# Feed-forward: the up projection as seven half-size products, and the down projection as a stage of its own

## The chip, the cores and the metric

One Trainium2 chip, one core. The metric is the device time of one execution in microseconds (us). TensorE is called PE in the profile, VectorE DVE, ScalarE ACT, GpSimd POOL; SP only starts DMAs. Every engine runs its own queue of instructions in order and waits on semaphores.

## The reference

One layer of a streaming encoder: attention with a compressed key/value cache, retention, and a feed-forward part. Only the last is touched. On 1152 tokens (1024 of one prompt, 8 x 16 of samples) of 1024 features, with 2816 hidden features:

```python
h = rms_norm(x, w['g_norm_ffn'])
u = h @ w['w_ffn_up']                       # 1024 -> 2 * 2816
# causal depthwise convolution over time, width 3, with bias, on all 5632 columns
gate, value = halves of the convolved u
x = x + (silu(gate) * value) @ w['w_ffn_down']   # 2816 -> 1024
```

The state of the convolution (the last two rows of `u` of the prompt and of each sample) is read and returned.

## The kernel before

Features lie on the 128 partitions, tokens along the free axis. A product in full precision is made of three products of rounded halves (`mm3`: high x high, high x low, low x high), so each weight tile and each activation row is split once by `split`: ScalarE casts to the high half (L205), VectorE subtracts (L206).

Attention, retention and the input projections come first. Then three layers of 8 output tiles each, `w_or`, `w_oa` and `w_out`, give the residual `xf[0..7]` (`ret_out`, `att_out`, `res_out`). Then the feed-forward part, a loop over 22 pairs `j`: gate tile `j` and value tile `22 + j`. For each of the two tiles:

- `up_mm` makes 3 token chunks x 8 k tiles x 3 = 72 products of 384 columns into three PSUM banks;
- `up_in` multiplies the sums by the norm's reciprocal root (row `iv2b`) as VectorE reads them out of PSUM (L1228, L1229), while POOL copies the convolution state in and out (L1224, L1225, L1230, L1231);
- `conv` starts on ScalarE (L1235) and takes two multiply-adds on VectorE (L1236, L1238), silu for the gate on ScalarE (L1240).

VectorE multiplies gate and value (L1305), the result is split into `ah` and `al`, and stays in SBUF. When two pairs are there, `down` multiplies them with their rows of `w_dn`: 8 output tiles x 3 chunks x 2 pairs x 3 products of 384 columns, each sum added to `xf` by VectorE (L1254, 264 additions). `down` for earlier pairs stands between the gate and the value products of a later one.

The order on each engine is that of the code as a scheduler of the tile framework lays it out by the dependencies; pools with a number of buffers set how far loads run ahead. Weights are loaded on SP's queue into `wraw`.

Of the kernel before, what the change touches and what calls it, by code (L numbers as in the profile page):

```python
# [8 lines left out]
F32 = mybir.dt.float32  # L9
F32R = mybir.dt.float32r  # L10
# [66 lines left out]
def _lay_out(x):  # L77
# [53 lines left out]
    o["w_dn"] = asc(a["w_ffn_down"][0].reshape(NJ, P, D))  # L131
# [41 lines left out]
def _body(tc, d):  # L173
# [37 lines left out]
    with ExitStack() as top:  # L211
        const = top.enter_context(pool("const"))
        dram = top.enter_context(pool("dram", space=bass.MemoryType.DRAM))
        wp = top.enter_context(pool("wp", bufs=4))
# [18 lines left out]
        s_r8 = scratch("s_r8", RH, (P, 256 + 2 * RV))  # L233
        stream = _Stream()
# [895 lines left out]
        rp = top.enter_context(pool("rrows", side=right))  # L1130

        def new_rows(mm, w, f0, f1, fill):
            wts = [wslot(d[w][f], D) for f in (f0, f1)]
            rows = []

            def row(k):
                hi = rp.tile([P, T], F32R, name="rh", tag=f"rh{k}")
                lo = rp.tile([P, T], F32R, name="rl", tag=f"rl{k}")
                fill(k, hi, lo)
                rows.append((hi, lo))  # L1140
                return hi, lo

            return rows, fm_pair(mm, wts, row)

        def layer(mm, w, n, fill, out):
            rows, first = new_rows(mm, w, 0, 1, fill)
            for f in range(n):
                out(f, fm_tile(mm, wslot(d[w][f], D), rows) if f > 1 else first[f])

        NU = 2 + SEQ + NB * (NS + 2)  # L1150
        fs = top.enter_context(pool("frows"))
        fw = top.enter_context(pool("fconv"))
        with ExitStack() as ph:
            mm = top.enter_context(pool("mm_f", bufs=6, space=PSUM))
            sm = top.enter_context(pool("sm_f", bufs=2, space=PSUM))
            wk = ph.enter_context(pool("mwork", bufs=2, side=right))
            ivb = rp.tile([P, T], F32, name="iv2b")
            xf = []

            def ret_out(f, ps):  # L1160
                xf.append(fs.tile([P, T], F32, name=f"xf{f}"))
                g = wk.tile([P, T], F32, name="mg")
                G.dma_start(g, s_gate[8 + f])
                for c in range(NCH):
                    cs = slice(c * CH, (c + 1) * CH)
                    V.tensor_tensor(out=xf[f][:, cs], in0=ps[c], in1=g[:, cs], op=ALU.mult)

            def att_out(f, ps):
                g = wk.tile([P, T], F32, name="mg")
                G.dma_start(g, s_gate[f])  # L1170
                for c in range(NCH):
                    cs = slice(c * CH, (c + 1) * CH)
                    V.tensor_tensor(out=g[:, cs], in0=ps[c], in1=g[:, cs], op=ALU.mult)
                    V.tensor_tensor(out=xf[f][:, cs], in0=xf[f][:, cs], in1=g[:, cs], op=ALU.add)

            acc = fw.tile([P, NU - 2], F32, name="cv")[:, :T]

            def res_out(f, ps):
                g = wk.tile([P, T], F32, name="mg")
                G.dma_start(g, d["x_fm"][f])  # L1180
                for c in range(NCH):
                    cs = slice(c * CH, (c + 1) * CH)
                    V.tensor_tensor(out=xf[f][:, cs], in0=ps[c], in1=g[:, cs], op=ALU.add)
                if f:
                    A.activation(g, xf[f], AF.Square)
                    V.tensor_tensor(out=acc, in0=acc, in1=g, op=ALU.add)
                else:
                    A.activation(acc, xf[f], AF.Square)

            layer(mm, "w_or", 8, lambda k, hi, lo: split(hi, lo, raw(s_ret[k], T)), ret_out)  # L1190
            layer(mm, "w_oa", 8, lambda k, hi, lo: split(hi, lo, raw(s_att[k], T)), att_out)
            layer(mm, "w_out", 8, lambda k, hi, lo: split(hi, lo, xf[k]), res_out)


            hr, (pg, pv) = new_rows(mm, "w_up", 0, NJ, lambda k, hi, lo: split(hi, lo, xf[k], gc(C_FFN, k)))


        with ExitStack() as ph:
            wk = ph.enter_context(pool("fwork", bufs=1))
            cn = cst("s_conv", (P, NF, 18), wk)  # L1200

            def up_mm(f):
                return fm_tile(mm, wslot(d["w_up"][f], D), hr)

            def up_raw(ps):
                u = wk.tile([P, NU], F32, name="u", bufs=2)
                us = u[:, 2 + SEQ:].rearrange("p (b c) -> p b c", b=NB)
                A.copy(u[:, 2:2 + CH], ps[0])
                V.tensor_copy(u[:, 2 + CH:2 + 2 * CH], ps[1])
                n = SEQ - 2 * CH  # L1210
                A.copy(u[:, 2 + 2 * CH:2 + SEQ], ps[2][:, :n])
                V.tensor_copy(us[:, :, 2:], ps[2][:, n:].rearrange("p (b i) -> p b i", b=NB))
                return u

            def up_in(f, ps, u=None):
                if u is None:
                    u = wk.tile([P, NU], F32, name="u", bufs=2)
                    us = u[:, 2 + SEQ:].rearrange("p (b c) -> p b c", b=NB)
                    tail = ps[2][:, SEQ - 2 * CH:].rearrange("p (b i) -> p b i", b=NB)
                else:  # L1220
                    us = u[:, 2 + SEQ:].rearrange("p (b c) -> p b c", b=NB)
                    ps = [u[:, 2 + c * CH:2 + (c + 1) * CH] for c in range(3)]
                    tail = us[:, :, 2:]
                G.tensor_copy(u[:, 0:2], cn[:, f, 0:2])  # L1224
                G.tensor_copy(us[:, :, 0:2], cn[:, f, 2:].rearrange("p (b i) -> p b i", b=NB))  # L1225
                for c in range(3):
                    n = min(CH, SEQ - c * CH)
                    V.tensor_tensor(out=u[:, 2 + c * CH:2 + c * CH + n], in0=ps[c][:, :n], in1=ivb[:, c * CH:c * CH + n], op=ALU.mult)  # L1228
                V.tensor_tensor(out=us[:, :, 2:], in0=tail, in1=ivb[:, SEQ:].rearrange("p (b i) -> p b i", b=NB), op=ALU.mult)  # L1229
                G.tensor_copy(cn[:, f, 0:2], u[:, SEQ:SEQ + 2])  # L1230
                G.tensor_copy(cn[:, f, 2:].rearrange("p (b i) -> p b i", b=NB), us[:, :, NS:])  # L1231
                return u

            def conv(f, u, c):
                A.activation(c, u[:, 2:], AF.Identity, scale=gc(C_CW, 2 * NF + f), bias=gc(C_CB, f))  # L1235
                V.scalar_tensor_tensor(out=c, in0=u[:, 1:NU - 1], scalar=gc(C_CW, NF + f), in1=c, op0=ALU.mult, op1=ALU.add)  # L1236
                yield 1
                V.scalar_tensor_tensor(out=c, in0=u[:, 0:NU - 2], scalar=gc(C_CW, f), in1=c, op0=ALU.mult, op1=ALU.add)  # L1238
                if f < NJ:
                    A.activation(c, c, AF.Silu)  # L1240

            def down(acts, wd, last):
                for f in range(8):
                    wts = [tuple(w[:, f * P:(f + 1) * P] for w in ww) for ww in wd]
                    if last and f == 7:
                        ps = [mm.tile([P, 512], F32, name="mm")[:, :CH] for _ in range(NCH)]
                    else:
                        ps = fm_tile(mm, wts, acts)
                    for c in range(NCH):
                        cs = slice(c * CH, (c + 1) * CH)  # L1250
                        if last and f == 7:
                            for k in range(2):
                                mm3(ps[c], wts[k], tuple(a[:, cs] for a in acts[k]), k == 0, k == 1)
                        V.tensor_tensor(out=xf[f][:, cs], in0=ps[c], in1=xf[f][:, cs], op=ALU.add)  # L1254
                        if last:
                            S.dma_start(d["y_fm"][f][:, cs], xf[f][:, cs])

            acts, wd = [], []
            held = [up_raw(p) for p in (pg, pv)]
            i2 = const.tile([P, NT], F32, name="i2")  # L1260

            def norm():
                V.tensor_scalar(out=ss, in0=col_sums(sm, acc), scalar1=1.0 / D, scalar2=EPS, op0=ALU.mult, op1=ALU.add)
                rpow(i2, ss)
                yield from to_rows(sm, ivb, i2, fw.tile([P, NU - 2], F32, name="cg")[:, :CH])

            def act_rows(cv, ah, al):
                split(ah[:, :SEQ], al[:, :SEQ], cv[:, :SEQ])
                sv = lambda a: a[:, SEQ:].rearrange("p (b i) -> p b i", b=NB)
# [3 lines left out]
            def down_w(j):  # L1273
                return wslot(d["w_dn"][j], D)
# [95 lines left out]
```

## Time and profile before

| | |
|---|---|
| median of 3 runs | 2465.95 us (2463.95 to 2468.12) |
| profiled execution | 2464.82 us; span 2463.0 us; granted clock 0.992 |
| PE busy | 2435.9 us, 99% of the span |
| DVE, ACT, POOL busy | 1319.5, 835.8, 302.3 us |
| bytes moved by DMA | 238.52 MB, mean 97 GB/s |

A busy time is the sum of an engine's instructions, not the time it was needed for. A group row reads: line, engine, operation, output <- inputs, shape, number; then total busy us and mean ns of one; then idle time of that engine ahead of the group and who ended it. A row of the chain reads: start, length, what ran, number of instructions. A row of the timeline reads: start, length, engine, line, operation.

### The profile page before, as it was taken

Reading aid. Unit: us, or ns where it says so; the run is one execution under the profiler, and the core shown is the slowest. Engines: PE = TensorE matmul, PEld = TensorE weight load, DVE = VectorE, ACT = ScalarE, POOL = GpSimd, SP = SyncE. Lnnn points to the kernel's source line nnn. Section 1 sums busy time; section 2 is a strip of 40 time slices with the busy share of each in tenths; the row PEclk is TensorE's granted clock in tenths of the full one; section 3 lists DMA queues with packets and bytes.
Section 4 is the critical chain, followed back from the end, with each engine's and each line's share of the span. In section 5 each row is a group of like instructions: output and inputs, shape, how many; then the busy total and the mean of one; then the engine's idle time right before and its main releaser. Section 6 shows DMA issues by size and latency. Waiting matters only on the chain.

```text
span 2463.0 us, 36197 instructions
## 1 busy us (share of the span) xinstructions
PE 2435.9 (99%) x14360; PEld 2333.8 (95%) x14360; DVE 1319.5 (54%) x2779; ACT 835.8 (34%) x2050; POOL 302.3 (12%) x514
## 2 busy tenths in 40 slices
PE   9999999999999999999999999999999999999999
PEld 9999998998999978887999999999999999999999
DVE  5223456456249856444886244247555555555555
ACT  5121332333236645664665022133221222212120
POOL 0001000001013302332110000011110101110010
PEclk9999999999999999998999999999999999999999
DMA  5332210220126576427764352210111111111102
GB/s 200 103 110 102 95 60 27 69 65 29 69 77 181 171 250 204 146 101 204 195 187 128 113 165 90 93 60 30 48 44 43 44 43 35 52 44 43 43 26 84
DMA packets 125273, 238.52 MB, mean 97 GB/s; under 512 B 10000, under 2 KB 73872, under 8 KB 124848
## 3 DMA queue, kind: packets, MB, share of 16 engines
q1 hardware_dynamic: 40320, 125.95, 15.6%
q10 hardware_dynamic: 58256, 62.30, 7.5%
q0 software_dynamic: 26528, 47.95, 7.0%
q8 instruction: 113, 1.85, 0.3%
q14 instruction: 56, 0.46, 0.1%
HBM read 168.76 MB, written 67.42 MB: 96 GB/s over the span
## 4 chain that ended last, share of the span: by engine, by line
PE 94%; DVE 3%; ACT 1%; DMA 1%; issue 1%; POOL 0%; ACTq 0%; SPq 0%; DVEq 0%; POOLq 0%
PE mm L188 81%; PE sm L188 4%; PE sc L188 3%; PE apo L188 2%; PE apt L1081 1%; DVE wlo L206 0%; DMA s<-s_ret 0%; PE sm L554 0%; DVE uqT L697 0%; DMA wraw<-w_gate 0%; PE sm L311 0%; PE sm L691 0%; PE sm L859 0%; DVE uqT L209 0%; PE sm L987 0%
## 5 line engine op out<-in xcount | busy, mean ns | idle before, releaser
L205 ACT CAST whi<-wraw 128x1024 fp32r<-128x1024 f32 (+2 forms) x165 | 172.3, 1053 | 725.8 <-PE mm L188 629.6
L188 PE MATMUL mm<-rh,whi 128*128 128x384 f32 x1728 | 392.7, 336 | 1.5 <-ACT rh L205 1.5
L188 PE MATMUL mm<-rh,wlo 128*128 128x384 f32 x1680 | 384.1, 336 | 0.0
L188 PE MATMUL mm<-rl,whi 128*128 128x384 f32 x1632 | 372.5, 336 | 0.1
L188 PEld LDWEIGHTS mm<-rh,whi 128*128 128x128 f32 x1728 | 308.1, 188 | 3.2 <-ACT rh L205 1.7
L188 PEld LDWEIGHTS mm<-rh,wlo 128*128 128x128 f32 x1680 | 300.2, 188 | 0.0
L188 PEld LDWEIGHTS mm<-rl,whi 128*128 128x128 f32 x1632 | 291.0, 188 | 0.4 <-DVE rl L206 0.4
L206 DVE TENSOR_TENSOR wlo<-wraw,whi 128x1024 fp32r<-128x1024 f32 (+2 forms) x165 | 200.1, 1222 | 142.1 <-ACT whi L205 142.0
L188 PE MATMUL mm<-whi,xh 128*128 128x256 f32 (+2 forms) x720 | 228.2, 333 | 0.7 <-DVE gsig L361 0.7
L188 PE MATMUL mm<-whi,xl 128*128 128x256 f32 (+2 forms) x720 | 225.3, 329 | 0.0
L188 PE MATMUL mm<-wlo,xh 128*128 128x256 f32 (+2 forms) x720 | 224.8, 329 | 0.2 <-DVE wlo L206 0.2
L1254 DVE TENSOR_TENSOR xf<-mm,xf 128x384 f32<-128x384 f32 x264 | 131.5, 551 | 86.2 <-PE mm L188 86.2
L1228 DVE TENSOR_TENSOR u<-mm,iv2b 128x384 f32<-128x384 f32 (+1 forms) x126 | 57.1, 507 | 208.9 <-PE mm L188 208.9
L188 PEld LDWEIGHTS mm<-whi,xl 128*128 128x128 f32 x720 | 132.5, 190 | 12.1
L188 PEld LDWEIGHTS mm<-whi,xh 128*128 128x128 f32 x720 | 132.6, 190 | 10.6 <-issue 0.7
L188 PEld LDWEIGHTS mm<-wlo,xh 128*128 128x128 f32 x720 | 132.6, 190 | 9.8 <-DVE wlo L206 0.4
L188 PE MATMUL mm<-xh,whi 128*128 128x384 f32 x528 | 123.9, 340 | 2.8 <-ACT whi L205 2.1
L188 PE MATMUL mm<-xl,whi 128*128 128x384 f32 x528 | 122.1, 337 | 0.0
L188 PE MATMUL mm<-xh,wlo 128*128 128x384 f32 x528 | 121.5, 336 | 0.0
L188 PE MATMUL mm<-ah,whi 128*128 128x384 f32 x480 | 110.4, 336 | 0.0
L188 PE MATMUL mm<-al,whi 128*128 128x384 f32 x480 | 110.4, 336 | 0.0
L188 PE MATMUL mm<-ah,wlo 128*128 128x384 f32 x480 | 109.7, 336 | 0.0
(448 smaller groups left out, 4449.0 us busy)
## 6 DMA issues: line engine op xcount, KB each, us to landing
wraw<-w_up SPq DMA_DIRECT2D x44, 512.0 KB, 3.2
s_q<-uqT ACTq DMA_DIRECT2D x36, 384.0 KB, 3.1
aq<-s_q POOLq DMA_DIRECT2D x8, 1536.0 KB, 9.1
wraw<-w_dn SPq DMA_DIRECT2D x22, 512.0 KB, 3.3
s_gate<-gsig ACTq DMA_DIRECT2D x16, 576.0 KB, 4.9
mg<-s_gate POOLq DMA_DIRECT2D x16, 576.0 KB, 5.0
wraw<-w_rqkv SPq DMA_DIRECT2D x16, 512.0 KB, 3.6
s_v<-kvT ACTq DMA_DIRECT2D x16, 512.0 KB, 4.6
```

The lines of the kernel that those rows point to most:

```text
L188: E.matmul(out, l, r, start=start, stop=stop)
L205: A.copy(hi, src)
L206: return V.tensor_tensor(out=lo, in0=src, in1=hi.bitcast(F32), op=ALU.subtract)
L1081: E.transpose(pt[:, j * 256 + e * P:j * 256 + (e + 1) * P], pm[e][:, jj * P:(jj + 1) * P], ident)
L1228: V.tensor_tensor(out=u[:, 2 + c * CH:2 + c * CH + n], in0=ps[c][:, :n], in1=ivb[:, c * CH:c * CH + n], op=ALU.mult)
L1254: V.tensor_tensor(out=xf[f][:, cs], in0=ps[c], in1=xf[f][:, cs], op=ALU.add)
```

## The change

Only the part from `w_or` on is changed, and the layout of `w_dn`.

**Up projection.** For one pair, gate and value tile are the two row blocks of a 2 x 2 block product; the 8 k tiles are halved into the two inner blocks, the 1152 tokens into two halves of 576. The four blocks of the result then come from seven products of half size (the Winograd form of Strassen's scheme) instead of eight: 7 products x 2 chunks of 288 columns x 4 k tiles x 3 = 168 products per pair (before: 144 of 384 columns). Three pairs of PSUM banks `p`, `q`, `r` hold the sums. A bank that has been read goes on summing the next product, and the reads in between give the four blocks (`read`). Four sums of weight blocks per pair are made by POOL (`up_w`); the sums of token blocks are made once, behind `w_out` (`res_out`, `combine`), whose tiles now come in the order 0, 4, 1, 5, 2, 6, 3, 7; ten blocks go through DRAM.

**Norm, convolution, gate.** Scaling by the norm (row `ivx`) is a step of POOL on SBUF, 1168 columns (`scaled`). The convolution is as before. The gated product goes to DRAM (`s_act`).

**Down projection.** After all 22 pairs: per chunk of 384 tokens and output tile, 66 products are summed in one PSUM bank (again 1584 products of 384 columns in all). Weights are loaded and split for each chunk anew (three times in all); activations are read back and split (66 tiles of 384). The residual comes from DRAM (`s_x`), 24 additions instead of 264.

Buffers: rows of `w_or` and `w_oa` come through 2 buffers instead of 3.

The core of the diff:

```diff
+        def up_w(j):
+            rg, rv = wraw(d["w_up"][j]), wraw(d["w_up"][NJ + j])
+            u, v = slice(0, 512), slice(512, D)
+            s = fwt.tile([P, D], F32, name="wsum", tag="ws")
+            wg = wtile(rg, D, 0)
+            G.tensor_tensor(out=s[:, v], in0=rg[:, u], in1=rv[:, u], op=ALU.add)
+            G.tensor_tensor(out=rv[:, u], in0=rv[:, u], in1=rv[:, v], op=ALU.add)
+            G.tensor_tensor(out=s[:, u], in0=rv[:, u], in1=rg[:, u], op=ALU.add)
+            G.tensor_tensor(out=rg[:, v], in0=s[:, u], in1=rg[:, v], op=ALU.add)
+            wa = wtile(s, D, 1)
+            wb = wtile(rv, D, 2)
+            wc = wtile(rg[:, v], 512, 3)
...
+        PRODUCTS = (("p", "a11", "b11", 1), ("q", "s2", "t2", 1), ("p", "a12", "b21", 0), ("q", "s3", "t3", 0),
+                    ("r", "s1", "t1", 1), ("q", "a22", "t4", 0), ("r", "s4", "b22", 0))
...
+                        for e, (l, x) in enumerate(((wh, xh), (wh, xl), (wl, xh))):
+                            E.matmul(banks[bank][c], l[:, ks], x, start=bool(first) and k + e == 0, stop=k + e == 5, skip_group_check=not first)
+                    read(n, c, banks[bank][c])
...
+                if n == 0:
+                    A.copy(r1[:, cs], ps)
+                elif n == 1:
+                    V.tensor_tensor(out=u2[:, cs], in0=r1[:, cs], in1=ps, op=ALU.subtract)
+                elif n == 2:
+                    A.copy(ug[:, us_], ps)
+                elif n == 3:
+                    V.tensor_tensor(out=u3[:, cs], in0=ps, in1=r1[:, cs], op=ALU.subtract)
+                elif n == 4:
+                    second(uv, c, ALU.subtract, u3, ps)
+                elif n == 5:
+                    V.tensor_tensor(out=uv[:, us_], in0=ps, in1=r1[:, cs], op=ALU.subtract)
+                else:
+                    second(ug, c, ALU.add, u2, ps)
...
+        def scaled(f, u):
+            us_ = samples(u)
+            G.tensor_copy(u[:, 0:2], cn[:, f, 0:2])
+            G.tensor_copy(us_[:, :, 0:2], cn[:, f, 2:].rearrange("p (b i) -> p b i", b=NB))
+            G.tensor_tensor(out=u[:, 2:], in0=u[:, 2:], in1=ivx[:, 2:], op=ALU.mult)
+            G.tensor_copy(cn[:, f, 0:2], u[:, SEQ:SEQ + 2])
+            G.tensor_copy(cn[:, f, 2:].rearrange("p (b i) -> p b i", b=NB), us_[:, :, NS:])
...
+        for j in range(NJ):
+            ug, uv = up(j, w)
...
+                w = up_w(j + 1)
+            scaled(NJ + j, uv)
+            conv(NJ + j, uv, cv)
+            scaled(j, ug)
+            conv(j, ug, cg)
+            A.activation(cg, cg, AF.Silu)
+            V.tensor_tensor(out=cv[:, :SEQ], in0=cg[:, :SEQ], in1=cv[:, :SEQ], op=ALU.mult)
...
+            A.dma_start(s_act[j][:, :SEQ], cv[:, :SEQ])
...
+            w, acts = down_w(0), down_a(0)
+            for c in range(NCH):
+                for f in range(8):
+                    for j in range(NJ):
+                        mm3(ps, w[j], acts[j], j == 0, j == NJ - 1)
+                    G.dma_start(x, s_x[f][:, cs])
+                    V.tensor_tensor(out=x, in0=ps, in1=x, op=ALU.add)
+                    S.dma_start(d["y_fm"][f][:, cs], x)
+                    if c * 8 + f < 23:
+                        w = down_w((f + 1) % 8)
```

`down_w` loads three pieces of 1024, 1024 and 768 columns (`dr`, one buffer each) and splits them into `dh` and `dl` (two buffers each); `down_a` loads 22 tiles of 384 columns on ScalarE's queue (`ar`, three buffers) and splits each into `act`.

How the order on the engines moves, at the places that the prediction speaks of. VectorE before, in the middle of the loop: `u` is read out of PSUM with the norm, `cv` and `cg` are the convolved value and gate, `al` the split of the gated product, `xf` the residual.

```order
L1229 TENSOR_TENSOR u_19937<-mm_19864,iv2b_14856 128x8x16
L206 TENSOR_TENSOR wlo_20253<-wraw_20250,whi_20252 128x1024
L1236 SCALAR_TENSOR_TENSOR cv_19946<-u_19937,c_gcol_112,cv_19946 128x1168
L1238 SCALAR_TENSOR_TENSOR cv_19946<-u_19937,c_gcol_112,cv_19946 128x1168
L1305 TENSOR_TENSOR cv_19946<-cg_19851,cv_19946 128x1168
L206 TENSOR_TENSOR al_19952<-cv_19946,ah_19951 128x1024
```

The convolution of one tile stands in one piece, and no step in it reads PSUM. VectorE now, from the reads of the sixth product of a pair on (`uv` and `ug` are value and gate, `u2` and `u3` partial results, `r1` the first product):

```order
L1359 TENSOR_TENSOR uv_22019<-mm_22052,r1_22020 128x288
L206 TENSOR_TENSOR wlo_22231<-wraw_22215,whi_22230 128x1024
L1338 TENSOR_TENSOR ug_22018<-u2_22021,mm_22131 128x288
L1376 SCALAR_TENSOR_TENSOR cv_22243<-uv_22019,c_gcol_154,cv_22243 128x1168
L1341 TENSOR_TENSOR ug_22018<-u2_22021,mm_22132 128x160
L1343 TENSOR_TENSOR ug_22018<-u2_22021,mm_22132 128x8x16
L206 TENSOR_TENSOR wlo_22235<-wraw_22213,whi_22234 128x512
L1377 SCALAR_TENSOR_TENSOR cv_22243<-uv_22019,c_gcol_154,cv_22243 128x1168
L1376 SCALAR_TENSOR_TENSOR cg_22252<-ug_22018,c_gcol_154,cg_22252 128x1168
L1351 TENSOR_TENSOR u2_22265<-r1_22264,mm_22295 128x288
L1377 SCALAR_TENSOR_TENSOR cg_22252<-ug_22018,c_gcol_154,cg_22252 128x1168
L1351 TENSOR_TENSOR u2_22265<-r1_22264,mm_22296 128x288
```

Reads of PSUM now stand between the convolution steps: the last reads of the gate behind the value's first step, and the reads of the next pair's second product (`u2_22265`) between the gate's steps. POOL before, copies of convolution state alone:

```order
L1224 COPY u_19735<-c_s_conv_17295 128x2
L1225 COPY u_19735<-c_s_conv_17295 128x8x2
L1230 COPY c_s_conv_17295<-u_19448 128x2
L1231 COPY c_s_conv_17295<-u_19448 128x16
L1224 COPY u_19842<-c_s_conv_17295 128x2
```

POOL now:

```order
L1283 TENSOR_TENSOR wsum_22461<-wraw_22457,wraw_22459 128x512
L1284 TENSOR_TENSOR wraw_22459<-wraw_22459 128x512
L1285 TENSOR_TENSOR wsum_22461<-wraw_22459,wraw_22457 128x512
L1368 COPY ug_22262<-c_s_conv_17320 128x2
L1369 COPY ug_22262<-c_s_conv_17320 128x8x2
L1286 TENSOR_TENSOR wraw_22457<-wsum_22461,wraw_22457 128x512
L1370 TENSOR_TENSOR uv_22263<-uv_22263,ivx_17319 128x1168
L1371 COPY c_s_conv_17320<-uv_22263 128x2
L1372 COPY c_s_conv_17320<-uv_22263 128x16
L1370 TENSOR_TENSOR ug_22262<-ug_22262,ivx_17319 128x1168
```

Six wide steps per pair have come in, the two scalings (L1370) behind the weight sums of the next pair. ScalarE before, at the end of the loop:

```order
L1240 ACTIVATE cg_23211<-cg_23211 128x1168
L205 CAST whi_23344<-wraw_23342 128x1024
L1235 ACTIVATE rh_23310<-u_23297,c_gcol_112 128x1168
L205 CAST rh_23308<-rh_23310 128x1024
L205 CAST rh_23308<-rh_23310 128x128
```

ScalarE now, at the same place, where the down stage begins (`dh` high halves of `w_dn`, `ar` and `act` activations read back):

```order
L1375 ACTIVATE cg_22715<-ug_22506,c_gcol_154 128x1168
L205 CAST dh_22740<-dr_22738 128x1024
L205 CAST dh_22746<-dr_22744 128x1024
L205 CAST dh_22752<-dr_22750 128x768
L1399 ACTIVATE cg_22715<-cg_22715 128x1168
L205 CAST dh_22939<-dr_22937 128x1024
L1404 DMA s_act21_140<-cv_22706 128x1024
L1405 DMA s_act21_140<-sa_22721 128x128
L205 CAST dh_22945<-dr_22943 128x1024
L205 CAST dh_22951<-dr_22949 128x768
L1432 DMA ar_22756<-s_act0_119 128x384
```

Six weight casts, the silu and two stores stand ahead of the first load of an activation.

375 lines of the change are left out of this document (216 added, 159 removed).

## The prediction, made before the changed kernel ran

> **What bounds the kernel now.** I read the page's first block and chain, then the longest waits of TensorE, then the chain piece by piece.
>
> ```profile
> span 2463.0 us, 36197 instructions
> PE 2435.9 (99%) x14360; PEld 2333.8 (95%) x14360; DVE 1319.5 (54%) x2779; ACT 835.8 (34%) x2050; POOL 302.3 (12%) x514
> PE 94%; DVE 3%; ACT 1%; DMA 1%; issue 1%; POOL 0%; ACTq 0%; SPq 0%; DVEq 0%; POOLq 0%
> PE sm L933 <- DVE rep L932: 3.8, 2, 2.7
> ...
> 204.47 6.40 PE mm L188 x48
> ...
> 1672.02 787.18 PE mm L188 x4536
> ```
>
> The reader is to see that TensorE is the whole story: 99% busy, 94% of the chain, and its worst wait of the program costs 3.8 us. The last row is almost all of the feed-forward part: 787.18 us without a break, 4536 products of 384 columns, so 173.5 ns each. The row of 48 products is from an earlier stage whose products have 288 columns, as one row of the timeline there shows; it gives 6.40 / 48 = 133.3 ns.
>
> ```profile
> 205.37 0.43 PE L188 MATMUL mm<-wlo,xh 128*128 128x288 f32 x2
> ```
>
> The profiled execution took 2464.8 us (span 2463.0 and 1.8 around it), 1.1 us below the median 2465.95 of the runs shown; the sum is made against 2464.8. About 5 us, 0.2%, is what a measurement of this kernel can tell from no change.
>
> **Part 1, the products.** Up projection before: 22 pairs x 144 products x 173.5 ns = 549.7 us. After: 22 x 168 x 133.3 = 492.7 us. The down projection keeps 1584 products of 384 columns, 274.8 us. So **-57.0 us** if TensorE stays the bound. One pair then lasts 168 x 133.3 = 22.4 us, and everything else in a pair must fit beneath that. No reason is seen for the shorter product to cost more than its row: weights are loaded as often per product there as here.
>
> **Part 2, what one pair asks of VectorE.** These groups are from the feed-forward window of before (and two from the whole run):
>
> ```profile
> L1254 DVE TENSOR_TENSOR xf<-mm,xf 128x384 f32<-128x384 f32 x264 | 131.5, 551 | 86.2 <-PE mm L188 86.2
> L206 DVE TENSOR_TENSOR wlo<-wraw,whi 128x1024 fp32r<-128x1024 f32 x60 | 73.0, 1216 | 10.9 <-ACT whi L205 10.9
> L1236 DVE SCALAR_TENSOR_TENSOR cg<-u,c_gcol,cg 128x1168 f32<-128x1168 f32 x22 | 31.5, 1432 | 5.0 <-ACT cg L1235 5.0
> L1305 DVE TENSOR_TENSOR cv<-cg,cv 128x1168 f32<-128x1168 f32 x21 | 28.9, 1375 | 0.7
> L206 DVE TENSOR_TENSOR al<-cv,ah 128x1024 fp32r<-128x1024 f32 x20 | 24.5, 1225 | 20.1 <-ACT ah L205 20.1
> L1228 DVE TENSOR_TENSOR u<-mm,iv2b 128x256 f32<-128x256 f32 x42 | 17.4, 415 | 0.0
> L1229 DVE TENSOR_TENSOR u<-mm,iv2b 128x128 f32<-128x128 f32 x42 | 11.8, 281 | 0.0
> ...
> L206 DVE TENSOR_TENSOR apT<-apt,apT 128x512 fp32r<-128x512 f32 x48 | 32.1, 685 | 5.2 <-ACT apT L205 5.2
> ```
>
> Weight splits: 3 x 1.22 + 0.69 = 4.3 us. Four convolution steps: 4 x 1.43 = 5.7. The gate product, 1024 and 128 columns: 1.23 + 0.28 = 1.5. Reads of the sums in PSUM: eight of 288 columns at about 0.45 (between the rows for 256 and 384 columns, 415 and 551 ns), and two pairs of 160 and 128 at 0.32 + 0.28: 4.8. Together 16.4 us, under 22.4. The 264 additions at L1254 (131.5 us) go away; that gains nothing, since TensorE did not wait for them. What VectorE does *not* do any more is the scaling by the norm, which is now two POOL products of 1168 columns; POOL also makes four weight sums of 512 columns per pair.
>
> **Part 3, POOL in the loop.** This is where the forecast is decided. Before has no wide POOL operation at all. Its rows and the same copies in time, with VectorE's operation beside each:
>
> ```profile
> L1231 POOL COPY c_s_conv<-u 128x16 f32<-128x16 f32 x44 | 45.0, 1022 | 0.8 <-DVE u L1229 0.3
> ...
> L1225 POOL COPY u<-c_s_conv 128x16 f32<-128x16 f32 x42 | 8.3, 198 | 0.0
> 1985.60 1.21 DVE L206 TENSOR_TENSOR wlo<-wraw,whi 128x1024 fp32r<-128x1024 f32 x1
> 1985.74 1.12 POOL L1231 COPY c_s_conv<-u 128x16 f32<-128x16 f32 x1
> ...
> 1990.14 1.38 DVE L1305 TENSOR_TENSOR cv<-cg,cv 128x1168 f32<-128x1168 f32 x1
> 1990.26 1.30 POOL L1224 COPY u<-c_s_conv 128x2 f32<-128x2 f32 x1 [3.39 <-DVE cv L1238]
> ...
> 2003.78 1.48 DVE L1254 TENSOR_TENSOR xf<-mm,xf 128x384 f32<-128x384 f32 x3
> 2004.02 0.19 POOL L1224 COPY u<-c_s_conv 128x2 f32<-128x2 f32 x1 [4.65 <-DVE cg L1238]
> ```
>
> The same small copy takes 0.2 us beside a VectorE operation that reads PSUM, and ends 0.05 us after a VectorE operation with two SBUF operands that was running when it began. POOL is held out. In the new loop 11.5 of VectorE's 16.4 us are such operations (splits, convolution, gate product).
>
> A wide POOL product is bounded below by VectorE's own row for the width, 1.38 us, and above by that plus one whole convolution step that holds it, 1.38 + 1.43 = 2.8. I take 2.6, because in VectorE's order a weight split (1.22) stands right behind the read that releases the value's scaling, and a half split and a convolution step (0.69, 1.43) right behind the one that releases the gate's. A weight sum is bounded in the same way by 0.69 and 0.69 + 1.22 = 1.9; I take 0.9 of VectorE's time for each, nearer the unheld end, since two of the four fall where VectorE is reading PSUM or waiting.
>
> VectorE works in order, and behind its steps there are now waits on POOL and ScalarE. ScalarE's rows:
>
> ```profile
> L205 ACT CAST whi<-wraw 128x1024 fp32r<-128x1024 f32 x60 | 63.0, 1050 | 371.6 <-PE mm L188 309.7 <-issue 61.9
> L1235 ACT ACTIVATE cg<-u,c_gcol 128x1168 f32<-128x1168 f32 x22 | 30.1, 1367 | 18.2 <-POOL c_s_conv L1230 16.9 <-DVE u L1229 1.3
> ...
> L1240 ACT ACTIVATE cg<-cg 128x1168 f32<-128x1168 f32 x22 | 26.0, 1182 | 74.4 <-DVE cg L1238 74.4
> ```
>
> Value half: after its last read, POOL 2.6 and ScalarE 1.37 pass before the first convolution step; VectorE fills 1.22 + 0.45 of that and waits 2.3. Behind that waiting step stand the gate's last reads, so the gate's scaling starts late too: 2.6 + 1.37, filled by 0.69 + 1.43, waits 1.9. The silu's 1.18 hides behind one read of 0.45: 0.7. Sum of waits 4.9. If POOL also holds VectorE out while it sums weights, 4 x 0.9 = 3.6 more. A pair then lasts 16.4 + 4.9 + 3.6 = 24.9 us, 2.5 over TensorE's 22.4: TensorE waits in the fourth product, whose bank VectorE reads between two convolution steps of the pair before. ScalarE's copy of the first product is queued behind the gate's convolution start in the same way, so the third product is late with it. 22 x 2.5 = **+55 us**. Bounds: 0 (waits and sums fit under 22.4) and, with sums of 1.4 each and each of the two long waits 1 us longer, 16.4 + 6.9 + 5.6 = 28.9, that is +143.
>
> What no row shows is POOL's own price. The Trainium skill, "GPSIMD Engine Reference", section 3.1, gives an fp32 tensor_tensor of 2048 elements 4497 ns on GpSimd against 2293 on VectorE; by it an estimate for 1168 is 2.6 us before any holding, against 1.38 in the row above. By the row alone, unheld, the pair fits under TensorE and the sum ends at 2434; by the page, with the holding added, it ends at the second rival's time. The skill's "SBUF — State Buffer", section "Who interferes with whom", calls the shared port an exclusive lock that blocks the loser fully. This trace agrees for POOL (1.12 and 1.30 us against 0.2); no row shows VectorE losing.
>
> **Part 4, from up to down.** Before, down products were interleaved, so nothing was exposed. Now ScalarE's order puts the last pair's tail, and all six weight casts of the first two tiles, ahead of the loads of the activations. From the last product of up: gate read 0.6, POOL 2.6, ScalarE 1.37, convolution step 1.43, a split 1.22, step 1.43 = 8.7; silu 1.18 beside two splits until 10.9; gate product 1.5 = 12.4. The second tile's weights reuse single raw buffers:
>
> ```profile
> wraw<-w_dn SPq DMA_DIRECT2D x22, 512.0 KB, 3.3
> y_fm<-xf SPq DMA_DIRECT2D x24, 192.0 KB, 2.0
> ```
>
> The middle piece is free at 9.9, loaded at 13.2, cast at 14.3; the third ends about 15.1. Only then is the first activation load issued, 192 KB: 2.0, and its cast about 0.5. TensorE starts at about 18. The 22 loads go through three buffers, (2.0 + 0.5 + 0.55) / 3 = 1.0 us each or a little more, while TensorE has 2 x 3 x 173.5 ns = 1.04 us per activation from two output tiles: about 2 more. **+20 us**, bounds 12 (POOL at 1.4 and the weight casts in time) and 33 (TensorE fed by one output tile only through 22 loads).
>
> **Part 5, the rest.** Down stage: per output tile TensorE 66 x 173.5 ns = 11.45 us. VectorE 2 x 1.22 + 0.95 + 0.55 + 2.75 x 0.55 = 5.5, ScalarE 4.3, three loads of up to 3.3; a raw buffer's round (3.3 + 1.05 + 1.22 = 5.6) fits. Cost 0; if loads took twice as long the round is still 8.9. The residual comes by POOL's queue, idle there, well ahead. Tail: an addition and a store as before, 0. Start of up: the last row's blocks (four subtractions or additions and a split of 576 columns, about 0.75 each, and two steps before) end 5 to 7 us after the last w_out product, against first products whose other three k tiles are ready (about 4 us with the copies): 3, bounds 0 and 6. The first layer's rows now come through two buffers and not three, loads of 5 us each: 3, bounds 0 and 6. Spilling and reloading ten blocks goes beside 72-product tiles of 12.5 us: 0. **+6 us.**
>
> Sum: 2464.8 - 57.0 + 55 + 20 + 6 = 2488.8, rounded **2489 us**, 0.9% slower.
>
> **Rivals.**
> *TensorE stays the bound (faster).* Place: the fourth product of each pair. If POOL's sums do not hold VectorE, the pair needs 16.4 + 4.9 = 21.3 us, under 22.4, and the stall is 0: 2464.8 - 57 + 26 = 2434. It decides at a pair of 22.4 + (57 - 26) / 22 = 23.8 us. For it: VectorE's rows sum to only 16.4, and no row shows VectorE held. Against: the copies that POOL finishes late, and an order in which every wide step of POOL has a two-operand step of VectorE right behind its release.
> *POOL is slow and also held.* If its products cost twice VectorE's row (2.75) and are held by 1.22 besides, each of the two chain pieces grows by 1.4: 24.9 + 2.8 = 27.7, 22 x 5.3 = 117: 2551. For it: POOL was held in most of its 44 copies (mean 1022 ns), and the skill's figure for GpSimd, named above, points the same way. Against: a POOL step that begins first would not be held.
> *The gains and losses cancel.* A pair of 23.6 to 24.0 us: within 5 us of 2465. Only a narrow band of the same cost.
> *Down starved by its loads.* 1 us per output tile would be 24 us, 2513; the rounds above speak against it.
>
> **How the numbers follow.** The forecast's mechanism, a pair of 24.0 to 26.3 us, 2470 to 2520: 0.42. TensorE bound or nearly so, 2422 to 2460: 0.34. Cancelled: 0.07. POOL slow and held, above 2520: 0.14, and down starved 0.03. Faster 0.34, same 0.07, slower 0.59. The range 2426 to 2540 leaves out about 0.03 below (transition at its lower bound and no stall) and 0.10 above; the worst sum of all bounds, 2464.8 - 57 + 143 + 33 + 12 = 2596, needs every one of them at once. The forecast's own case alone is 2470 to 2520.
>
> **What would show it.** Products of up at 133 ns in unbroken pieces, POOL's 1168 products at 2.6 us or more, TensorE's waits named after the reads at L1351 and the copy at L1349, pieces of up lasting 25 us per pair, and a hole of about 18 us before the first product on act. It is wrong if POOL's wide rows come near 1.4 us, or if TensorE's 3696 products of up run without a break.

## The result, and the profile after

The changed kernel took 2497.65 us (median of 4 runs, 2494.53 to 2502.61) against 2464.95: ratio 1.0133, 95% interval 1.0113 to 1.0154. The forecast was 2489. The sum came out near; its terms did not, as the ledger below shows.

First block of the page of the changed kernel, then the chain's shares by engine:

```profile
span 2495.5 us, 38305 instructions
PE 2398.6 (96%) x14888; PEld 2278.9 (91%) x14888; DVE 1488.1 (60%) x2792; ACT 961.9 (39%) x2294; POOL 605.0 (24%) x678
...
PE 76%; DVE 10%; ACT 4%; DMA 4%; issue 4%; POOL 3%; ACTq 0%; SPq 0%; POOLq 0%; DVEq 0%
```

TensorE was 99% busy and 94% of the chain; it is 96% and 76% now. Its longest waits (line <- who released it: total us, times, longest us):

```profile
PE mm L188 <- ACT act L205: 26.9, 5, 24.9
PE sc L188 <- ACT ap L1069: 14.8, 2, 14.2
PE mm L1308 <- DVE u L1351: 10.8, 20, 0.6
PE mm L1308 <- ACT r L1349: 9.6, 21, 1.7
PE sm L315 <- DVE acc L1234: 5.0, 1, 5.0
```

Before, nothing was longer than 2.8 us at a time. The first two rows are holes that come once (24.9 and 14.2 us), the next two short waits that come in every pair, the last a single wait at the start of up. Pieces of the chain show how long a pair is, and where TensorE runs unbroken again:

```profile
1741.98 8.28 PE mm L1308 x59
1765.86 8.28 PE mm L1308 x59
...
2236.97 255.01 PE mm L188 x1467
```

From one pair to the next it is 23.88 us; 168 products of 133.3 ns would be 22.4. The marks for the ledger are rows of TensorE's timeline: first product of `w_or` before and now, first product of up, last of up and first of down now, last of down now and before:

```profile
1329.16 1.34 PE L188 MATMUL mm<-rh,whi 128*128 128x384 f32 x6 [1.51 <-ACT rh L205]
...
1343.34 0.97 PE L188 MATMUL mm<-rh,whi 128*128 128x384 f32 x4 [2.01 <-ACT rh L205]
1645.49 0.42 PE L1308 MATMUL mm<-xb,whi 128*128 128x288 f32 x2
2183.96 0.29 PE L1308 MATMUL mm<-xb,wlo 128*128 128x288 f32 x1
2209.16 1.28 PE L188 MATMUL mm<-act,dh 128*128 128x384 f32 x2 [24.91 <-ACT act L205]
2491.63 0.34 PE L188 MATMUL mm<-act,dl 128*128 128x384 f32 x1
...
2458.85 0.34 PE L188 MATMUL mm<-rh,wlo 128*128 128x384 f32 x1
```

| term, us | forecast | measured | from |
|---|---|---|---|
| fewer product columns | -57 | -57 | 549.7 - 492.7, taken over; the unbroken piece of the first experiment gives 132.5 ns per product |
| pair longer than TensorE's work | +55 | +31 | 21 x (23.88 - 22.4) |
| start of up | +3 | +12 | up 538.8 (1645.49 to 2184.25) - 492.7 - 31, less the 3.4 that up and down of before, with the norm's products, took beyond 4752 x 173.5 ns |
| up to down, and starving after | +20 | +33 | hole 24.9; down 282.8 instead of 274.8 |
| start of `w_or` | +3 | +14 | 1343.34 - 1329.16 |
| sum | +24 | +33 | spans: 2495.5 - 2463.0 = 32.5 |

The start of `w_or` is off by a hole that lies ahead of attention, 180 us earlier. The sum is near because errors of both signs cancel: -24 on the pair, +33 on the other three terms. POOL's and VectorE's groups in the changed kernel (mean ns behind the comma):

```profile
L1370 POOL TENSOR_TENSOR ug<-ug,ivx 128x1168 f32<-128x1168 f32 x22 | 67.6, 3072 | 49.8 <-DVE ug L1343 49.8
L1370 POOL TENSOR_TENSOR uv<-uv,ivx 128x1168 f32<-128x1168 f32 x22 | 60.8, 2762 | 74.3 <-DVE uv L1359 74.3
L1283 POOL TENSOR_TENSOR wsum<-wraw 128x512 f32<-128x512 f32 x22 | 49.3, 2243 | 10.1 <-DMA wraw<-w_up 10.1
L1286 POOL TENSOR_TENSOR wraw<-wsum,wraw 128x512 f32<-128x512 f32 x22 | 28.9, 1313 | 29.1 <-DVE wlo L206 29.1
...
L206 DVE TENSOR_TENSOR wlo<-wraw,whi 128x1024 fp32r<-128x1024 f32 x42 | 94.6, 2253 | 9.8 <-ACT whi L205 9.8
L1377 DVE SCALAR_TENSOR_TENSOR cv<-uv,c_gcol,cv 128x1168 f32<-128x1168 f32 x22 | 83.3, 3787 | 0.0
L1400 DVE TENSOR_TENSOR cv<-cg,cv 128x1024 f32<-128x1024 f32 x22 | 49.5, 2250 | 18.5 <-ACT cg L1399 18.5
L1377 DVE SCALAR_TENSOR_TENSOR cg<-ug,c_gcol,cg 128x1168 f32<-128x1168 f32 x22 | 45.0, 2045 | 0.0
```

VectorE's steps themselves have become longer: the split 2.25 instead of 1.22 us in the mean of two per pair, the second convolution step 3.79 and 2.05 instead of 1.43, the gate product 2.25 instead of 1.23. In time, one split and one convolution step beside POOL's two scalings:

```profile
1822.60 2.72 POOL L1370 TENSOR_TENSOR uv<-uv,ivx 128x1168 f32<-128x1168 f32 x1 [3.03 <-DVE uv L1359]
1823.01 3.39 DVE L206 TENSOR_TENSOR wlo<-wraw,whi 128x1024 fp32r<-128x1024 f32 x1 [0.49 <-ACT whi L205]
...
1828.77 3.04 POOL L1370 TENSOR_TENSOR ug<-ug,ivx 128x1168 f32<-128x1168 f32 x1 [2.18 <-DVE ug L1343]
1829.14 3.90 DVE L1377 SCALAR_TENSOR_TENSOR cv<-uv,c_gcol,cv 128x1168 f32<-128x1168 f32 x1
```

The split ends at 1826.40, 1.08 us after POOL's product (1825.32), which is about its own unheld time (1.21 for the pair's other split): while POOL worked, it hardly advanced. The convolution step ends 1.23 us after POOL's second product. So VectorE loses when POOL is first, which no row of before could show. The Trainium skill ("SBUF — State Buffer", section "Who interferes with whom") says that the loser of the shared port blocks fully; these rows agree, in the direction that the prediction left open. The other direction is here too: two of the four weight sums on POOL, 1.29 us when undisturbed, take 2.3 us (the row at L1283). POOL's own price for 1168 columns is 2.72 us when it goes first; the estimate from "GPSIMD Engine Reference", section 3.1, of the Trainium skill was 2.6.

The two holes, in time. Ahead of attention (`whi` is the first weight of `w_or`, `ap` the first softmax):

```profile
1149.20 0.39 ACTq L1044 DMA_DIRECT2D s_att<-wraw  x1
1159.00 1.04 ACT L205 CAST whi<-wraw 128x1024 fp32r<-128x1024 f32 x1 [10.28 <-DMA s_att<-wraw]
...
1162.45 1.04 ACT L205 CAST whi<-wraw 128x1024 fp32r<-128x1024 f32 x1 [2.40 <-DMA wraw<-w_or]
...
1165.22 0.37 ACT L1069 ACTIVATE ap<-sc,ast 128x128 f32<-128x128 f32 x1 [1.73 <-DVE ast L1062]
```

A store out of one of the old raw-weight buffers takes 9.8 us, while the DMA engines move 346 GB/s, most of it loads on POOL's queue for attention. The first cast of `w_or` waits for it, and so does the load of the second weight: their buffers are laid over the one being stored. Both casts stand in ScalarE's queue ahead of the first softmax. Between up and down:

```profile
2187.63 1.43 DVE L1377 SCALAR_TENSOR_TENSOR cv<-uv,c_gcol,cv 128x1168 f32<-128x1168 f32 x1
...
2187.86 3.70 POOL L1370 TENSOR_TENSOR ug<-ug,ivx 128x1168 f32<-128x1168 f32 x1 [3.06 <-DVE ug L1343]
...
2203.43 0.83 ACT L205 CAST dh<-dr 128x768 fp32r<-128x768 f32 x1 [0.67 <-DMA dr<-w_dn]
2203.44 1.34 ACTq L1432 DMA_DIRECT2D ar<-s_act  x3
...
2208.59 0.51 ACT L205 CAST act<-ar 128x384 fp32r<-128x384 f32 x1 [4.33 <-DMA ar<-s_act]
```

Last product of up at 2184.25, loads issued at 2203.4 behind the sixth weight cast (the prediction's working gave 15.1 us after the last product, it was 19.2), 5 us until the first is there (2.0 was put). POOL's last scaling took 3.70 us instead of 2.72: here VectorE's step was first, by 0.23 us, and POOL was held.

The long waits also cost time behind them. Stretches of the trace behind the 5.0 us wait at the start of up, behind the hole before down, and after that (stretch, length, busy us and instructions of PE, PEld, DVE, ACT and POOL, then granted TensorE clock, DMA share, GB/s):

```profile
1661.60:1668.50 6.90, 6.90 (x31) 6.90 (x32) 1.75 (x5) 0.98 (x3) 2.61 (x4) 0.50 0.01 5
2209.16:2218.55 9.39, 8.32 (x20) 5.95 (x21) 3.27 (x6) 2.90 (x6) 0.00 (x0) 0.51 0.62 206
2218.55:2237.00 18.45, 17.56 (x99) 16.50 (x98) 8.25 (x14) 7.49 (x15) 0.00 (x0) 1.00 0.55 173
```

In the 9.39 us behind the hole, at a granted clock of 0.51, TensorE made 20 products (3.5 us at 173.5 ns each) and waited 1.1 us. So about 5 of the 8.0 us that down took too long (282.8 against 274.8) went to slow products; all waits for activations behind the hole are 2.0 us (26.9 - 24.9). At the start of up, 18 products of the norm and the next 15 of up lost 3.5 us in the same way. No term of the sum has this cost; why the clock is lower there, the rows do not show.

### The profile page after: what moved, and what is told of

It is laid out like the page before. It is cut to its first block, busy times and chain, and to the rows that moved or that the text cites. A ratio compares the mean times of both kernels' runs of the same rounds, so it can differ in the third digit from the quotient of the medians.

```text
span 2495.5 us, 38305 instructions
## 1 busy us (share of the span) xinstructions
PE 2398.6 (96%) x14888; PEld 2278.9 (91%) x14888; DVE 1488.1 (60%) x2792; ACT 961.9 (39%) x2294; POOL 605.0 (24%) x678
## 4 chain that ended last, share of the span: by engine, by line
PE 76%; DVE 10%; ACT 4%; DMA 4%; issue 4%; POOL 3%; ACTq 0%; SPq 0%; POOLq 0%; DVEq 0%
PE mm L188 56%; PE mm L1308 7%; PE sm L188 4%; PE sc L188 3%; POOL ug L1370 3%; PE apo L188 2%; DVE cg L1377 2%; DVE wlo L206 1%; DVE cv L1376 1%; PE apt L1085 1%; ACT whi L205 1%; DVE cg L1376 1%; ACT cg L1375 1%; DMA ar<-s_act 1%; DMA s<-s_ret 1%
## 5 line engine op out<-in xcount | busy, mean ns | idle before, releaser
L1308 PE MATMUL mm<-xt,whi 128*128 128x288 f32 x1408 | 287.5, 298 | 11.9 <-DVE u L1351 10.8
L188 PE MATMUL mm<-act,dh 128*128 128x384 f32 x1056 | 272.2, 338 | 26.9 <-ACT act L205 26.9
L1308 PEld LDWEIGHTS mm<-xt,whi 128*128 128x128 f32 x1408 | 224.6, 188 | 20.0 <-DVE u L1351 15.4
L1308 PE MATMUL mm<-xb,whi 128*128 128x288 f32 x1056 | 215.6, 298 | 9.6 <-ACT r L1349 9.6
L188 PEld LDWEIGHTS mm<-act,dh 128*128 128x128 f32 x1056 | 192.3, 189 | 30.9 <-ACT act L205 29.2
L1308 PE MATMUL mm<-xt,wlo 128*128 128x288 f32 x704 | 207.8, 295 | 0.0
L1308 PEld LDWEIGHTS mm<-xb,whi 128*128 128x128 f32 x1056 | 170.2, 189 | 14.7 <-ACT r L1349 14.4
L188 PE MATMUL mm<-act,dl 128*128 128x384 f32 x528 | 177.2, 337 | 0.0
L188 PEld LDWEIGHTS mm<-whi,xl 128*128 128x128 f32 x720 | 132.7, 190 | 12.1
L188 PEld LDWEIGHTS mm<-whi,xh 128*128 128x128 f32 x720 | 132.8, 190 | 10.5 <-issue 0.7
L188 PE MATMUL mm<-rh,whi 128*128 128x384 f32 x576 | 131.9, 336 | 2.0 <-ACT rh L205 2.0
L188 PE MATMUL mm<-rl,whi 128*128 128x384 f32 x576 | 132.1, 336 | 0.4 <-DVE rl L206 0.4
L188 PE MATMUL mm<-rh,wlo 128*128 128x384 f32 x576 | 131.5, 335 | 0.0
```

Of the source, the lines that this page charges most:

```text
L188: E.matmul(out, l, r, start=start, stop=stop)
L1308: E.matmul(banks[bank][c], l[:, ks], x, start=bool(first) and k + e == 0, stop=k + e == 5, skip_group_check=not first)
```

## The experiments

Two theories on the pair of 23.88 us: **hold** (POOL's wide steps and VectorE's two-operand steps shut each other out, and VectorE's queue with its held steps sets the pair), against **latency** (two POOL steps stand on the chain from pair to pair, VectorE itself has room). Then the holes, and the two halves of the change. The recorded expectations name the runs by labels: experiments 1 to 10 here are e1, e2, e9, e3, e6, e4, e5, e8, e7 and e10.

**1. Scaling on VectorE.**

```diff
-            G.tensor_tensor(out=u[:, 2:], in0=u[:, 2:], in1=ivx[:, 2:], op=ALU.mult)
+            V.tensor_tensor(out=u[:, 2:], in0=u[:, 2:], in1=ivx[:, 2:], op=ALU.mult)
```

> The two products of 1168 columns per pair that scale by the norm run on VectorE instead of POOL; all else as in the changed kernel (2497.65 us, 23.88 us per pair in the steady part of up). Theory (POOL's wide steps and VectorE's two-operand steps shut each other out, and VectorE with its held steps sets the pair): VectorE takes on 2 x 1.38 = 2.8 us per pair but loses the 4.6 us that its split and its second convolution step stood held beside the scalings (3.39 against 1.22, 3.89 against 1.43), and the chain loses two POOL steps of 2.7; the pair falls to 22.4 to 22.7, TensorE's own time, about -28 us, and the tail behind the last pair is some 4 us shorter: 2462 to 2470. Rival (VectorE is simply full with its own work): 2.8 us more per pair, up to +60 us: 2525 to 2560. Rival (only the weight sums hold it): no change within 5 us.

2460.35 us: 37 less, just below the theory's range, and under the kernel before (0.9981, interval 0.9971 to 0.9990). The chain has one piece for nearly all of up, and VectorE's steps have their old length where POOL scaled (split, second convolution step):

```profile
1681.19 472.77 PE mm L1308 x3568
...
L206 DVE TENSOR_TENSOR wlo<-wraw,whi 128x1024 fp32r<-128x1024 f32 x42 | 51.0, 1213 | 0.0
L1377 DVE SCALAR_TENSOR_TENSOR cv<-uv,c_gcol,cv 128x1168 f32<-128x1168 f32 x22 | 31.4, 1429 | 0.0
```

472.77 / 3568 = 132.5 ns: TensorE is the bound again, at the price that the prediction took. "VectorE is simply full" falls: it does more and the pair is shorter. Hold and latency would both do this.

**2. No weight sums.** The four sums on POOL are left out, so the splits read other numbers.

```diff
-            G.tensor_tensor(out=s[:, v], in0=rg[:, u], in1=rv[:, u], op=ALU.add)
-            ... (three more)
-            wa = wtile(s, D, 1)
+            wa = wtile(rg, D, 1)
```

> The four weight sums per pair on POOL are left out (the splits read the loaded weights instead, so the products are of other numbers); the scalings stay on POOL. Theory (exclusive hold, VectorE sets the pair): what the sums hold VectorE (second gate step 2.10 against 1.43, gate product 2.35 against 1.23, one split 1.56 against 1.22, together 2.1 us) goes away, the pair falls from 23.88 to about 22.4, -25 to -33 us: 2465 to 2473. Rival (the chain through the two scalings alone sets the pair, VectorE's holds do not matter): at most -5 us: 2492 to 2498.

2479.02 us, 18.6 less: between the two. A pair (pieces of the chain) is 23.08 us, and the convolution step beside the scaling is as long as ever:

```profile
1714.69 11.40 PE mm L1303 x83
1737.77 11.40 PE mm L1303 x83
...
L1372 DVE SCALAR_TENSOR_TENSOR cv<-uv,c_gcol,cv 128x1168 f32<-128x1168 f32 x21 | 81.6, 3884 | 0.0
```

0.8 of the 2.1 us of holds by the sums counted; the rest became idle time of VectorE, which is busy 19.9 of the 23.08 us here and 21.9 of the 23.88 in the changed kernel. The two scalings alone keep the pair over 22.4, and with a VectorE that is not full. The first pair is 4.7 us shorter too (36.4 to 31.7): the wait for `acc` at the start of up, 5.0 us in the changed kernel, is 0.7.

**3. POOL's work off the chain.** Experiment 1, with two POOL products per pair that nothing waits for:

```diff
             V.tensor_tensor(out=u[:, 2:], in0=u[:, 2:], in1=ivx[:, 2:], op=ALU.mult)
+            G.tensor_tensor(out=spare[:, 2:], in0=u[:, 2:], in1=ivx[:, 2:], op=ALU.mult)
```

> As e1_scale_on_dve (2460.35 us, VectorE scales), and POOL does two more products of 1168 columns per pair into a spare tile that nothing reads, right behind VectorE's scaling, so that POOL's work is that of the changed kernel but no step waits for these two. Theory (POOL's and VectorE's steps shut each other out, VectorE too): VectorE's own 19.2 us per pair plus holds of 4.6 and 2.1 us give 24.5 to 26.6 us per pair, 2505 to 2550. Rival (only the two POOL steps on the chain from one pair to the next made the pair long; VectorE is not held or has room): the pair stays at 22.4, 2457 to 2465.

2535.32 us, 75 more than experiment 1. Rows in time, one pair apart, of the product that waits for VectorE, and VectorE's step beside the spare product:

```profile
1775.25 0.54 PE L1308 MATMUL mm<-xt,whi 128*128 128x288 f32 x2 [1.55 <-DVE u L1352]
...
1800.98 0.53 PE L1308 MATMUL mm<-xt,whi 128*128 128x288 f32 x2 [1.54 <-DVE u L1352]
...
1795.56 3.77 POOL L1372 TENSOR_TENSOR spare<-ug,ivx 128x1168 f32<-128x1168 f32 x1 [3.63 <-DVE ug L1371]
...
1797.05 3.52 DVE L1378 SCALAR_TENSOR_TENSOR cg<-ug,c_gcol,cg 128x1168 f32<-128x1168 f32 x1
```

25.73 us per pair, of which VectorE is busy 24.4. No step waits for the spare product, yet VectorE's convolution step took 3.52 us instead of 1.43, and TensorE waited for VectorE. Latency falls as the whole cause; hold is shown. How the 23.88 us of the changed kernel divide between the two stays open: VectorE is idle for 2.0 us of a pair there, and in experiment 2 the chain through the two scalings, with its held steps, set a pair of 23.08.

**4 and 5. The hole ahead of attention.** Once other buffers laid over the store's buffer, and once the first two splits of `w_or` moved in the queue:

```diff
+        for i in (3, 2):
+            for t in "hl":
+                fwt.tile([P, sizes[i]], F32R, name="whi" if t == "h" else "wlo", tag=f"{t}{i}")
+        fwt.tile([P, D], F32, name="wsum", tag="ws")
```

> Only the places of the weight buffers in SBUF change: the tiles that w_or does not use first are laid over the region of the old raw-weight buffers, so that the first two w_or loads no longer wait for the slow store out of one of them. Theory (the 14 us hole ahead of attention is ScalarE's first w_or cast, queued ahead of the first softmax and waiting for a load that waits for that store): hole gone but for 1 or 2 us, -11 to -14 us: 2483 to 2487. Rival (attention starts late for another reason, as the store's traffic itself): unchanged, 2495 to 2500.

2495.47 us: only 2.2 less, within the rival's range and the spread of the runs. The hole was cut to 6.9 us, with a second wait of 2.5, not away: the load no longer waited for the store, but ran beside it and beside POOL's loads, and ScalarE's queue waited for the load:

```profile
PE sc L188 <- ACT ap L1069: 9.4, 2, 6.9
...
1155.76 1.04 ACT L205 CAST whi<-wraw 128x1024 fp32r<-128x1024 f32 x1 [4.48 <-DMA wraw<-w_or]
```

```diff
+                if h == 6:
+                    mid = [...]   (cut: the last ScalarE and VectorE instruction ahead of head 6)
...
+            if w == "w_or":
+                with tc.issue_after(mid[0]), tc.issue_after(mid[1]):
+                    wts = [bslot(d[w][f]) for f in (f0, f1)]
```

> As the changed kernel (2497.65 us), but the first two w_or splits on ScalarE and VectorE stand behind the start of attention head 6 instead of ahead of the first softmax. Theory (the 14 us hole before attention is those casts waiting in ScalarE's queue; e3 only shortened the load's wait, as the load itself then ran beside the slow store and took 6.8 us): the hole goes to 0 or 1 us, -12 to -15 us: 2482 to 2486. Rival (the slow store holds attention in another way, or the loads miss the start of w_or): 2491 or more.

2489.04 us, 8.6 less, short of 12. The hole is gone, and the first product of `w_or` came 10.8 us earlier than in the changed kernel:

```profile
1332.54 0.97 PE L188 MATMUL mm<-rh,whi 128*128 128x384 f32 x4 [2.01 <-ACT rh L205]
```

So the casts' place in the queue was the cause. From the first score product of attention to `w_or` the trace is 14.7 us shorter, but that first product came 3.9 us later (1152.01 and not 1148.14). Its start lies between 1148.14 and 1155.71 in traces of kernels whose code is the same up to there, so the missing part can be spread.

**6 and 7. The hole before down.** Activations first, loads on POOL's queue with six buffers:

```diff
-                    r = dx.tile([P, CH], F32, name="ar")
-                    A.dma_start(r, s_act[j][:, c * CH:(c + 1) * CH])
+                    r = dx.tile([P, CH], F32, name="ar", bufs=6)
+                    G.dma_start(r, s_act[j][:, c * CH:(c + 1) * CH])
...
+                        with tc.issue_after(subs[5].ins), tc.issue_after(casts[5].ins):
                             w = down_w((f + 1) % 8)
```

> At the start of the down stage the second output tile's weights are queued behind the first six activation tiles on ScalarE and VectorE, and the activation loads go on POOL's queue with six buffers instead of ScalarE's with three. Theory (the 25 us hole and the 8 us lost behind it are the weight casts and reloads queued ahead of the loads, and the three buffers): first down product about 15 us after the last up product instead of 25, and less starving behind it: -10 to -17 us: 2481 to 2488. Rival (the hole is the last pair's own tail through POOL, convolution, silu and store, 16 us that no order of loads can shorten, and then TensorE starves without the second tile's weights): -3 to +5 us: 2494 to 2503.

2496.44 us: nothing won, within the rival's range. TensorE's first product comes sooner, and then it waits again:

```profile
PE mm L188 <- ACT act L1434: 26.4, 4, 17.5
...
2205.75 1.28 PE L188 MATMUL mm<-act,dh 128*128 128x384 f32 x2 [5.18 <-ACT act L1434]
```

POOL's second load waited 12.8 us, until the last store of an activation had landed: its buffer lay over the convolution's work tiles. So in the next the buffers were laid over the up weights instead, with the same loads but without the new order of the weights, on top of experiment 1:

```diff
-            dw = ph.enter_context(pool("dwt", bufs=2))
-            da = ph.enter_context(pool("dact", bufs=2))
             dx = ph.enter_context(pool("dmisc", bufs=3))
+            dw = ph.enter_context(pool("dwt", bufs=2))
+            da = ph.enter_context(pool("dact", bufs=2))
```

> As e1_scale_on_dve (2460.35 us), and the activation loads of the down stage go on POOL's queue with six buffers, from buffers laid over the up weights instead of over the convolution's work tiles. Theory (the hole of 20.7 us before down and the 8 us behind it come from loads that are issued late and three buffers): loads are there when ScalarE gets to them, hole about 16, starving behind it about 4: -5 to -9 us against e1: 2451 to 2455. Rival (ScalarE's order, six weight casts and the silu ahead of the first activation cast, sets the hole): within 3 us of e1: 2457 to 2463.

2458.19 us, 2.2 under experiment 1: within the rival's 3. The first six activations are there in time, and the hole is still 17.8 us (20.7 in experiment 1): their casts stand behind the six weight casts. ScalarE's order holds the hole.

**8. One half alone: plain up, the new down.**

```diff
-            ug, uv = up(j, w)
+            pg, pv = first_pair if j == 0 else (fm_tile(mm, bslot(d["w_up"][f]), hr) for f in (j, NJ + j))
+            ug, uv = up_one(j, pg, j == 0), up_one(NJ + j, pv, j == 0)   # L1228's form: read and scale out of PSUM
```

> One half of the change alone: the up projection in the plain form of before (144 products of 384 columns per pair, scaled by VectorE as it reads PSUM, no weight sums, no token blocks), with activations through DRAM and down as a stage of its own, as in the changed kernel. By the account so far the seven products bring -57 + 46 = -11 us net, and all the rest of the change costs 14 (hole before attention) + 25 + 8 (start of down) = 47 less about 4 (no POOL scaling in the tail): before + 43 = 2503 to 2511, slower than the changed kernel. Rival (the hole before down belongs to the seven products, whose last pair has the long tail): hole under 15 us and 2485 to 2497.

2505.93 us, in the account's range; the seven products alone are worth 8 us here, with POOL in their loop. But the hole is the rival's:

```profile
PE mm L188 <- ACT act L205: 14.4, 4, 12.1
```

12 us, not 25: half of the hole before down belongs to the seven-product form, whose last pair has reads, scaling and convolution of two tiles behind its last product (about 4 of the 13 us are POOL's scaling: the hole is 20.7 in experiment 1). The account put 21 for this hole, so its total is met in part by luck: in the trace the later start of `w_or` (15.7), the hole (12.1) and the loss behind it (8.9) make most of 39 us.

**9 and 10. Together.** Experiments 1, 5 and 7 (those of this numbering: scaling, head 6, early loads), then also the weights of the second down tile behind six activations, as in 6.

> Scaling on VectorE (e1), the early activation loads (e5) and the w_or splits behind head 6 (e6) together. If the terms lie in different stages and add: -37 (e1, measured), -12 to -15 (e6) and -5 to -9 (e5) from 2497.65: 2437 to 2444, about 1% under the kernel before. Rival (a gap closed early is given back at the next stage): 2448 or more.

2443.94 us, ratio 0.9919 (0.9903 to 0.9936): at the upper edge of the forecast. The differences that were measured one by one (37.3, 8.6 and 2.2) would add to 2449.6; the 5.6 us beyond them are not taken apart.

> As e7_all (2443.94 us), and the second down tile's weights stand behind the first six activation tiles on ScalarE and VectorE. Theory (with the loads early and six buffers, the weight casts are what is left of the hole beyond the last pair's tail): the hole before down falls from 18.3 to about 11 us: 2436 to 2440. Rival (as in e4: what is won in the hole is lost waiting for the second tile's weights): 2442 to 2448.

2439.68 us, ratio 0.9900 (0.9880 to 0.9920), 1% under the kernel before. The order that was worth nothing in 6 is worth 4 us where the loads are early:

```profile
PE mm L188 <- ACT act L1440: 15.4, 3, 13.2
```

The hole is still 13.2 us and was forecast to 11, from 18.3; the trace of experiment 9 has 15.7. Of the 4 us, 2.5 are the hole, and down itself is 2.9 shorter (280.0 against 283.0).

## Why the prediction was right, point by point

- **Bound and direction.** Right: TensorE's price was there (132.5 ns per product in experiment 1), and the pair was set by VectorE and POOL. Waits named after L1351 and L1349 are the ones forecast.
- **POOL's price.** Taken at 2.6 with VectorE's row and a hold; it is 2.72 with no hold at all, 3.07 with. Right size, wrong make-up: POOL is slow by itself, and it is mostly VectorE that is held by it. Where VectorE was first, POOL was held as forecast (3.70 at the end of up).
- **The pair, 24.9 forecast, 23.88 measured: the mis-sized term** (+55 against +31). The step that failed is the adding of 4.9 us of waits and 3.6 of holds as two things. By the rows, holds are 6.4 us per pair: 2.1 on the split beside the value's scaling, 2.35 and 0.61 on the second convolution steps, 1.02 on the gate product, 0.3 on the split of the sum. The scalings' holds, 4.4 of these, were put at nothing. While VectorE is held in a split, ScalarE's convolution start passes beneath it; a hold and a wait on the same POOL step are one piece of time. VectorE is busy 21.9 of the 23.88 us, so 2.0 are left for waits, and its own work is 15.5 where 16.4 was put.
- **Up to down, 20 forecast, 33 measured.** The chain of steps was right, and so was the queue; mis-sized were POOL's last scaling (3.7, held), the reloads behind it (the loads issued 19.2 and not 15.1 us in) and the first load (5 us for 2.0, beside weight loads). The 2 us of waits behind the hole came as forecast (2.0); the term left out is TensorE's half clock there, about 5 us.
- **Start of up, 3 against 12.** The wait of 5.0 us for `acc` in TensorE's queue (L315) was not in the account, nor the 3.5 us at half clock behind it. Without POOL's weight sums the wait is 0.7 (experiment 2). The other 3 to 4 us were not taken apart.
- **Start of `w_or`, 3 against 14.** Not foreseen. The working looked at the rows' buffers; what cost the time was a weight buffer laid over one that a slow store was still reading, and a cast queued in front of attention. The order of ScalarE would have shown the cast, and the trace of before the store: it took 10.5 us there (1152.43 to 1162.91), with nothing waiting for it.
- **Rivals.** "TensorE stays the bound" would have been right as to the pair with the scaling on VectorE (2460 with the other losses left). "POOL slow and held" did not come at its size, since where POOL is first it is VectorE that pays. "The gains and losses cancel" has the measured pair: 23.88 lies in its 23.6 to 24.0, below the 24.0 to 26.3 of the forecast's own mechanism.

So the number was right by luck. The errors had both signs, -24 on the pair and +33 on the three edges; with the pair that came, the prediction's own sum says no change, and the kernel is slower only because the edges cost +59 where +26 was put.

## What to carry to other kernels

A step given to POOL is not off VectorE's books: count its length against the VectorE steps with two operands in SBUF that fall beside it. Here 2.75 us more on VectorE was cheaper than 5.8 on POOL. A stage of its own costs at its edges, where queues hold the next stage's first steps behind the last one's, and here each hole was followed by some us of TensorE at half clock: look for what stands ahead of the first load in each in-order queue, and for which buffer lies over which. And the reordered queue paid here only where the loads behind it were already early (0 us in one setting, 4 in the other).

## What was not expected of the hardware

A store of 128 x 8 x 128 floats took 9.8 us (1149.20 to 1159.00; 10.5 in the kernel before), and a weight load beside it 6.8 where it took 3.4 behind it. Loads on POOL's queue ran beside the store and beside that load, so neither 9.8 nor 6.8 is the transfer's own price. VectorE's steps that read PSUM kept their length beside POOL's wide steps (0.44 to 0.46 us for 288 columns throughout). TensorE's granted clock was about 0.50 for 2 us or more behind each of the waits of 5.0, 14.2 and 24.9 us, and 1.00 again within 10 us.
